# Turned keys copied ahead of the exponents, the merge spread through the last projection of the scan branch, and its buffers placed anew

## The chip, the cores and the metric

The kernel runs on one core of one Trainium2 chip. Five engines share the work: TensorE (PE) does the matrix products, VectorE (DVE), ScalarE (ACT) and GpSimd (POOL) do the elementwise work, and SyncE (SP) issues most transfers; ACT and POOL can issue transfers too, each on a queue of its own. The metric is the device time of one execution in microseconds. The kernel before takes 1907.57 us, the median of three runs from 1902.23 to 1909.16.

## The reference

One layer of a hybrid decoder: 512 prompt tokens and 64 sample tokens (8 sequences of 8) go through the same weights, each group with its own past. Cut to what matters here:

```python
h = x + 0.5 * swiglu(rmsnorm(x))                      # FFN 1
z, xbc, dt, q, k, v, f, g_ssd, g_att = split(rmsnorm(h) @ w_in)
y_ssd = ssd_branch(z, xbc, dt, ...)                   # conv, scan, gate, norm: 4 groups of 512 channels
y_att = fox_attention(q, k, v, f)                     # with a paged cache of 2048 keys a sequence
merged = sigmoid(g_ssd) * (y_ssd @ w_ssd_proj) + sigmoid(g_att) * (y_att @ w_attn_proj)
h = h + merged @ w_out
y = h + 0.5 * swiglu(rmsnorm(h))                      # FFN 2
```

The outputs are y and the new keys, values, forget logs, scan states and conv rows of both groups.

## The kernel before

**Tiles.** All 576 tokens are worked on together, and an activation is kept turned: 8 tiles of 128 channels by 576 tokens. A product is made column tile by column tile (`j`, 128 output channels) and in two halves of 288 tokens. Each operand is split into a high and a low part, so one product is three matmuls for every 128 rows of the weight (`mm3`, L208 to L210: high times high, high times low, low times high). Weights arrive by SP's queue in tiles `stage` (512 KB, four buffers); `split` makes `whi` on ACT (L173) and `wlo` on DVE, or on POOL at every `share[0]`-th time (L174). Activations are split by `hilo`: the high part on ACT (L217), the low part on DVE (L218).

**What sets the order.** The program is written in one sequence and a scheduler orders each engine's instructions by a timeline model of its own; what stands in a `soon()` block gets a higher priority. An engine then runs its instructions in that fixed order and waits wherever an operand is not there. Pools of buffers ("left" and "right" side of the on-chip memory) tie later tiles to the release of earlier ones.

**Stages.** FFN 1; the input projection; the attention, whose sample part turns gathered keys on PE and copies them out of PSUM on ACT (`turn_keys`, L907 and L908: `kT`), in turn with ACT's exponents (L850 for the prompt); then four groups of the scan branch. A group has its conv tiles (`conv_tile`, buffers `xr`), its scan (`group_scan`, which leaves the gated result split in `ygh` and `ygl`), and its projection:

`group_out(g)` multiplies the group's four channel tiles by 512 rows of `w_ssd_proj`: for each of 8 columns and 2 halves 12 matmuls into a PSUM tile `acc` (two banks), then `u = acc * rg` on DVE (L1378) and `accs[j] += u` (L1380; on POOL in groups 1 and 2, on DVE in group 3). `accs0` to `accs7` are the running sums over the groups, 128x576 each. `gate_tile` leaves the gates of the scan branch in DRAM (`thD`), three of them behind group 0's scan and five behind group 3's. The attention's gated projection lies in DRAM too (`mattD`), as does the residual (`hD`).

**The merge**, behind the last `group_out` (L1397 to L1424). For each column it loads the gate `th` on SP's queue (L1403) and the attention part `mt` on ACT's queue (L1405), makes `th = (th + 1) * accs[j]` on DVE (L1406), adds `mt` on POOL (L1407; on DVE for the last column) and splits the sum into `mh` and `ml`. Every one of these tiles lies in a pool that opens when the pools of the scan have closed. The eight residual tiles `h` are loaded on ACT's queue (L1410) into a pool of their own. Then `w_out`: 384 matmuls (8 columns, 2 halves, 8 row tiles, 3 each) that use `mh` and `ml`, and `h = 0.5 * acc + h` on DVE (L1421). For these, PSUM tiles are taken from `acc` and `pv` by turns, so four are there, and the scheduler lets the first four halves (columns 0 and 1) run abreast: they take the row tiles `mh0`, `mh1`, ... in the order in which these are made, and cannot end before the last of the eight is there. FFN 2 follows, with the norm of the new `h`.

Of the kernel before, what the change touches and what calls it, by code (L numbers as in the profile page):

```python
# [93 lines left out]
def build(ctx, tc, A, O):  # L94
# [8 lines left out]
    def pool(name, bufs=1, **kw):  # L103
        return tc.tile_pool(name=name, bufs=bufs, **kw)
# [534 lines left out]
    with pool("att", side="right", reuse_waits="tile") as ap:  # L639
# [242 lines left out]
        class Sample:  # L882
# [17 lines left out]
            def turn_keys(self, jq):  # L900
                kk = self.kk.pop(jq)
                self.kT = []
                for p in range(2):
                    self.kT.append(tl(ap, [P, 512], tag="kT", bufs=2))
                    t = tr()
                    for i in range(4):
                        nc.tensor.transpose(t[:, i * P:(i + 1) * P], kk[:, i, p * P:(p + 1) * P], ident)  # L907
                    act(self.kT[p], t, AF.Copy)  # L908

            def q(self, kv):  # L910
                return qz[:, kv // 2, self.b, kv % 2].rearrange("d g t -> d (g t)")
# [184 lines left out]
                G.tensor_copy(yt[p * 4 + g][:, NP:], ys[:, p, g, :])  # L1096


    xzs = ExitStack()
    xz = xzs.enter_context(pool("xz", side="right", reuse_waits="tile"))  # L1100

# [1 line left out]

    def conv_tile(ct, w, prev, out):

        xr = tl(xz, XR, tag="xr", bufs=2)
        xsamp = xr[:, 3 + NP:]
        xsamp = xsamp.rearrange("p (b u) -> p b u", u=T + 3)
        G.memset(xr[:, :3], 0.0)
        G.tensor_copy(xsamp[:, :, :3], prev.rearrange("p (j b) -> p b j", b=B))  # L1110
        a = acc()
        mm3(a, w, xs, 0)
        with soon():
            V.tensor_tensor(xr[:, 3:3 + HT], a, rbc[:, hs(0)], ALU.mult)
        full = tl(accp, [P, 512], tag="acc")
        a = full[:, :HT]
        mm3(a, w, xs, 1)
        with soon():
            V.tensor_tensor(xr[:, 3 + HT:3 + NP], a[:, :NP - HT], rbc[:, HT:NP], ALU.mult)
        with soon():  # L1120
            V.tensor_tensor(xsamp[:, :, 3:], a[:, NP - HT:].rearrange("p (b t) -> p b t", t=T),
                            rbc[:, NP:].rearrange("p (b t) -> p b t", t=T), ALU.mult)

        n = 3 + (T + 3) * B
        with soon():
            t = full[:n, 512 - P:]
            nc.tensor.transpose(t, xr[:, NP:], ident)
            tt = tl(xz, [n, P], tag="tt", bufs=1)
            act(tt, t, AF.Copy)  # L1129
        nc.scalar.dma_start(out=O["conv_p"][0, 0, :, ct * P:(ct + 1) * P], in_=tt[:3])  # L1130
        for j in range(3):
            r = 3 + T + j
            nc.scalar.dma_start(out=O["conv_s"][0, :, j, ct * P:(ct + 1) * P], in_=tt[r:r + (T + 3) * (B - 1) + 1:T + 3])

        m = NP + B * (T + 3)
        cv = tl(mixp, XR, tag="kf", bufs=2)
        wc = lambda j: P2[:, j * 24 + ct:j * 24 + ct + 1]
        act(cv[:, :m], xr[:, :m], AF.Identity, bias=P1[:, 40 + ct:41 + ct], scale=wc(0))
        for j in range(1, 4):
            V.scalar_tensor_tensor(cv[:, :m], xr[:, j:j + m], wc(j), cv[:, :m], ALU.mult, ALU.add)  # L1140
        act(xr[:, :m], cv[:, :m], AF.Tanh)
        V.scalar_tensor_tensor(out[:, :NP], xr[:, :NP], 1.0, cv[:, :NP], ALU.add, ALU.mult)
        samples = lambda v: v[:, NP + 3:].rearrange("p (b u) -> p b u", u=T + 3)[:, :, :T]
        V.scalar_tensor_tensor(out[:, NP:].rearrange("p (b t) -> p b t", t=T), samples(xr), 1.0, samples(cv), ALU.add, ALU.mult)
# [44 lines left out]
                nc.scalar.dma_start(out=mattD[:, j, :], in_=mt)  # L1189


    sa = mixes.enter_context(pool("ssdacc", reuse_waits="tile"))
    with xzs, pool("ssd", side="right", reuse_waits="tile") as wk:
        accs = [tl(sa, [P, NT], tag=f"accs{j}") for j in range(8)]
        cz = tl(wk, [P, B, 32], tag="cz")
        lastb = tl(wk, [P, 5, 32], tag="x4", bufs=3)
# [10 lines left out]
        def group_scan(g, bT, cT, xg):  # L1207
# [21 lines left out]
            def halves(half):  # L1229

                for i in range(4):
                    if half == 0:
                        yhl.append((tl(wk, [P, NT], F32R, tag="ygh", bufs=4), tl(wk, [P, NT], F32R, tag="ygl", bufs=4)))
                    w = P1[:, 24 + 4 * g + i:25 + 4 * g + i]
                    hi, lo = yhl[i][0][:, hs(half)], yhl[i][1][:, hs(half)]
                    act(hi, xg[:, i, hs(half)], AF.Copy, scale=w)
                    V.scalar_tensor_tensor(lo, xg[:, i, hs(half)], w, hi.bitcast(F32), ALU.mult, ALU.subtract)
# [126 lines left out]
        def group_out(g, ysq, ys_):  # L1364
# [3 lines left out]
            for j in range(8):  # L1368
                w = cw.get(j)
                for half in range(2):  # L1370
                    a = acc()
                    mm3(a, w, ys_, half)
                    if g == 0:
                        with soon():
                            V.tensor_tensor(accs[j][:, hs(half)], a, rg[:, hs(half)], ALU.mult)
                    else:
                        u = tl(wk, [P, HT], tag="u", bufs=2)
                        V.tensor_tensor(u, a, rg[:, hs(half)], ALU.mult)  # L1378
                        E = V if g == 3 else G
                        E.tensor_tensor(accs[j][:, hs(half)], accs[j][:, hs(half)], u, ALU.add)  # L1380

        gs = Cols(win, CGS)
        late = iter(range(8))
        for g in range(4):
# [5 lines left out]
            for _ in range((3, 0, 0, 5)[g]):  # L1390
                j = next(late)
                gate_tile(gs, j, 8 + j)
            group_out(g, *gated)


    hp2 = ctx.enter_context(pool("h2", side="right", reuse_waits="tile"))
    hts = [tl(hp2, [P, NT], tag=f"h{k}") for k in range(8)]  # L1397
    with mixes:
        with pool("mhl", bufs=8, side="right", reuse_waits="tile") as mp, pool("mg", side="right", reuse_waits="tile") as mg:
            mhl = []  # L1400
            for j in range(8):
                th = tl(mg, [P, NT], tag="th", bufs=3)
                nc.sync.dma_start(out=th, in_=thD[:, 8 + j, :])  # L1403
                mt = tl(mg, [P, NT], tag="mt", bufs=3)
                nc.scalar.dma_start(out=mt, in_=mattD[:, j, :])  # L1405
                V.scalar_tensor_tensor(th, th, 1.0, accs[j], ALU.add, ALU.mult)  # L1406
                (G if j < 7 else V).tensor_tensor(th, th, mt, ALU.add)  # L1407
                mhl.append(hilo(mp, th, "mh", "ml"))
            for j in range(8):
                nc.scalar.dma_start(out=hts[j], in_=hD[:, j, :])  # L1410
            wide[0] = True
            co = Cols(A["w_out"][0], 0)
            nrm3 = Norm(16, mg)
            for j in range(8):
                w = co.get(j)
                for half in range(2):
                    a = acc()
                    mm3(a, w, mhl, half)
                    hv = hts[j][:, hs(half)]
                    with soon():  # L1420
                        V.scalar_tensor_tensor(hv, a, 0.5, hv, ALU.mult, ALU.add)  # L1421
                nrm3.add(hts[j])
            nrm3.finish()
            share[0] = 0  # L1424


    with pool("out", bufs=2, reuse_waits="tile") as op:
# [48 lines left out]
```

## Time and profile before

| | value |
|---|---|
| median of three runs | 1907.57 us |
| the profiled execution's own time | 1901.34 us |
| its span, first to last instruction | 1899.5 us |
| last projection of the scan branch, merge, first four halves of `w_out` | 1367 to 1440 us in the span |
| FFN 2 behind it | to the end of the span |

A row of the timeline has the start in us from the span's start, the duration, the engine, the source line, the operation, what is written and read, and in brackets the idle time ahead of it and what ended that. A row by groups has line, engine, operation, operands and count, then the busy time and the mean nanoseconds of one, then the idle time ahead of the group's instructions and who ended it. A row of windows has the stretch and its length, the busy time of PE, of PE's weight loads, DVE, ACT and POOL with the number of instructions, the clock that TensorE was granted (1.00 is full), the busy share of the transfer engines and the bytes moved. The chain is followed back from the last instruction to whatever released each step; its rows give the idle time in us, the count and the longest one.

### The profile page before, as it was taken

How to read it: one execution, taken by the hardware profiler on the slowest of the kernel's cores; microseconds unless marked ns; L12 is line 12 of the kernel's file. 1: busy time of each engine (PE TensorE's matmuls, PEld its weight loads, DVE VectorE, ACT ScalarE, POOL GpSimd, SP SyncE). 2: the span in 40 equal slices, each digit the busy share in tenths (PEclk: the TensorE clock that was granted, in tenths of full speed). 3: DMA queues.
4: the chain of work that ended last, by engine and by line, in shares of the span. 5: the costliest groups of instructions: out<-in, count | busy, mean ns of one | idle time of the engine just before them, and what ended most of it. 6: DMA issues, size and time to landing. Idle time of an engine off the chain costs nothing.

```text
span 1899.5 us, 38775 instructions
## 1 busy us (share of the span) xinstructions
PE 1843.6 (97%) x15335; PEld 1738.3 (92%) x15335; DVE 1061.9 (56%) x2308; ACT 745.5 (39%) x1545; POOL 603.7 (32%) x678
## 2 busy tenths in 40 slices
PE   7999999999999999999899999999979999999999
PEld 7999999999899888888898898888979999999998
DVE  5544234443425677776746968787665545445442
ACT  4233223333323555554425645555423333223322
POOL 0432002312312334433224644747434322102210
PEclk9999999999998999999999999999989999999999
DMA  5453443444625678785456445344543444444432
GB/s 153 111 142 123 134 128 118 122 140 140 158 80 147 187 225 244 213 227 155 115 134 190 148 126 144 104 133 123 165 144 109 132 128 139 132 139 123 121 116 69
DMA packets 298235, 269.71 MB, mean 142 GB/s; under 512 B 55068, under 2 KB 262092, under 8 KB 297900
## 3 DMA queue, kind: packets, MB, share of 16 engines
q1 hardware_dynamic: 230864, 186.52, 35.0%
q10 hardware_dynamic: 57828, 46.09, 7.9%
q0 software_dynamic: 9360, 34.61, 5.9%
q8 instruction: 121, 1.98, 0.4%
q14 instruction: 62, 0.51, 0.1%
HBM read 223.71 MB, written 38.73 MB: 138 GB/s over the span
## 4 chain that ended last, share of the span: by engine, by line
PE 85%; DVE 5%; DMA 4%; ACT 3%; issue 1%; POOL 1%; ACTq 1%; SPq 0%; POOLq 0%; DVEq 0%
PE acc L208 17%; PE acc L209 16%; PE acc L210 16%; PE pv L209 7%; PE pv L208 7%; PE pv L210 7%; PE tr L917 2%; PE tr L907 1%; PE mm L844 1%; DMA ab<-cumD 1%; PE pv L875 1%; PE mm L862 1%; PE pv L1299 1%; DVE kf L1140 1%; PE pv L955 1%
## 5 line engine op out<-in xcount | busy, mean ns | idle before, releaser
L173 ACT ACTIVATE whi<-stage 128x512 fp32r<-128x512 f32 (+2 forms) x474 | 294.8, 622 | 739.4 <-PE acc L209 650.5
L208 PE MATMUL acc<-xh,whi 128*128 128x288 f32 x1792 | 544.7, 304 | 9.0 <-ACT tt L1129 3.8
L209 PE MATMUL acc<-xl,whi 128*128 128x288 f32 x1792 | 535.8, 299 | 0.0
L210 PE MATMUL acc<-xh,wlo 128*128 128x288 f32 x1792 | 535.0, 299 | 0.0
L174 DVE TENSOR_TENSOR wlo<-stage,whi 128x512 fp32r<-128x512 f32 (+1 forms) x373 | 261.1, 700 | 263.3 <-ACT whi L173 249.4
L208 PEld LDWEIGHTS acc<-xh,whi 128*128 128x128 f32 x1792 | 341.1, 190 | 15.4 <-ACT tt L1129 6.7
L209 PEld LDWEIGHTS acc<-xl,whi 128*128 128x128 f32 x1792 | 341.3, 190 | 1.9 <-issue 1.4
L210 PEld LDWEIGHTS acc<-xh,wlo 128*128 128x128 f32 x1792 | 340.7, 190 | 1.8 <-issue 1.2
L174 POOL TENSOR_TENSOR wlo<-stage,whi 128x512 fp32r<-128x512 f32 (+1 forms) x101 | 138.2, 1368 | 315.8 <-ACT whi L173 300.4
L341 POOL TENSOR_TENSOR u<-u,s 128x288 f32<-128x288 f32 x88 | 81.3, 924 | 425.6 <-DVE u L340 379.9
L208 PE MATMUL pv<-xh,whi 128*128 128x288 f32 (+1 forms) x720 | 214.1, 298 | 1.0 <-ACT xh L220 0.9
L209 PE MATMUL pv<-xl,whi 128*128 128x288 f32 (+1 forms) x720 | 212.9, 296 | 0.0
L210 PE MATMUL pv<-xh,wlo 128*128 128x288 f32 (+1 forms) x720 | 212.4, 295 | 0.0
L208 PEld LDWEIGHTS pv<-xh,whi 128*128 128x128 f32 (+1 forms) x720 | 135.1, 188 | 1.7 <-ACT xh L220 1.1
L209 PEld LDWEIGHTS pv<-xl,whi 128*128 128x128 f32 (+1 forms) x720 | 135.1, 188 | 1.2
L210 PEld LDWEIGHTS pv<-xh,wlo 128*128 128x128 f32 (+1 forms) x720 | 135.0, 188 | 0.2
L208 PE MATMUL pv<-hh,whi 128*128 128x288 f32 x352 | 105.7, 300 | 0.0
L343 POOL TENSOR_TENSOR hl<-u,hh 128x288 fp32r<-128x288 f32 x88 | 79.1, 901 | 80.7 <-ACT hh L342 80.7
L208 PE MATMUL acc<-hh,whi 128*128 128x288 f32 x352 | 104.1, 296 | 0.0
L209 PE MATMUL pv<-hl,whi 128*128 128x288 f32 x352 | 104.0, 296 | 0.0
L210 PE MATMUL acc<-hh,wlo 128*128 128x288 f32 x352 | 104.0, 296 | 0.0
L209 PE MATMUL acc<-hl,whi 128*128 128x288 f32 x352 | 104.0, 295 | 0.0
(346 smaller groups left out, 3622.5 us busy)
## 6 DMA issues: line engine op xcount, KB each, us to landing
stage<-in_w_in_dram SPq DMA_DIRECT2D x52, 512.0 KB
stage<-in_ffn_w_up_dram SPq DMA_DIRECT2D x44, 512.0 KB
stage<-in_ffn_w_gate_dram SPq DMA_DIRECT2D x43, 512.0 KB
stage<-in_ffn_w_down_dram SPq DMA_DIRECT2D x40, 512.0 KB
h<-in_state_ssm_dram SPq DMA_DIRECT2D x64, 256.0 KB
hTD<-hT ACTq DMA_DIRECT2D x32, 256.0 KB
pb<-pastD SPq DMA_DIRECT2D x32, 256.0 KB
ab<-cumD SPq DMA_DIRECT2D x32, 256.0 KB
```

The lines of the kernel that those rows point to most:

```text
L173: act(hi, view, AF.Copy)
L174: e.tensor_tensor(lo, view, hi.bitcast(F32), ALU.subtract)
L208: mm(out, lhsT=hi, rhs=a, start=first and i == 0, stop=False)
L209: mm(out, lhsT=hi, rhs=b, start=False, stop=False)
L210: mm(out, lhsT=lo, rhs=a, start=False, stop=last and i == n - 1)
L341: G.tensor_tensor(u, u, sil[half], ALU.mult)
L343: G.tensor_tensor(hl[:, hs(half)], u, hh[:, hs(half)].bitcast(F32), ALU.subtract)
L844: mm(s[:, :n], lhsT=q, rhs=ks[2 * self.p + e][:, :n], start=hl == 0, stop=hl == 1)
L862: nc.tensor.transpose(t[:, j * P:(j + 1) * P], lt[:, j * P:(j + 1) * P], ident)
L875: mm(self.ob[o:o + 32, i * P:(i + 1) * P], lhsT=vtok[j][:, v0:v0 + 32], rhs=self.pts[e][:, j * P:(j + 1) * P], start=j == 0, stop=j == i)
L907: nc.tensor.transpose(t[:, i * P:(i + 1) * P], kk[:, i, p * P:(p + 1) * P], ident)
L917: mm(s[kv * 32:(kv + 1) * 32, :], lhsT=self.q(kv), rhs=self.kT[kv // 2], start=True, stop=True)
```

## The change

Four things.

1. The copies `kT` are written under `soon()`.
2. The sums `accs` and the row sums `ssq` move into a pool `sums` on the right side that opens before the conv's pool and stays to the end. The pool of the projection's operands (`outs`: `ygh`, `ygl`, `u`) is split from the scan's and lives as long as the conv's pool. `xr` has three buffers, not two.
3. The gates and attention parts are loaded into the conv's old tiles (`bT`, `cT` and `xr`), both on ACT's queue, and those of columns 0 and 1 are asked for ahead of the last `group_out`. As the merge needs no new pool but the one of `mh` and `ml`, the scheduler is free to set a column's merge between later columns of the projection.
4. The residual tiles take the places of the sums: `h` for column j is loaded into `accs[j]`'s place when the merge has read it, on POOL's queue, behind the addition of that column.

The lines of the change have new numbers: the merge's two elementwise operations are L1415 and L1416, the loads L1387, L1389 and L1419, `u` and the sums L1380 and L1382, the residual's addition L1430.

```diff
--- before.py
+++ after.py
@@ -905,7 +905,8 @@
                     t = tr()
                     for i in range(4):
                         nc.tensor.transpose(t[:, i * P:(i + 1) * P], kk[:, i, p * P:(p + 1) * P], ident)
-                    act(self.kT[p], t, AF.Copy)
+                    with soon():
+                        act(self.kT[p], t, AF.Copy)
 
             def q(self, kv):
                 return qz[:, kv // 2, self.b, kv % 2].rearrange("d g t -> d (g t)")
@@ -1096,6 +1097,7 @@
                 G.tensor_copy(yt[p * 4 + g][:, NP:], ys[:, p, g, :])
 
 
+    sa = ctx.enter_context(pool("sums", side="right", reuse_waits="tile"))
     xzs = ExitStack()
     xz = xzs.enter_context(pool("xz", side="right", reuse_waits="tile"))
 
@@ -1103,7 +1105,7 @@
 
     def conv_tile(ct, w, prev, out):
 
-        xr = tl(xz, XR, tag="xr", bufs=2)
+        xr = tl(xz, XR, tag="xr", bufs=3)
         xsamp = xr[:, 3 + NP:]
         xsamp = xsamp.rearrange("p (b u) -> p b u", u=T + 3)
         G.memset(xr[:, :3], 0.0)
@@ -1189,8 +1191,8 @@
                 nc.scalar.dma_start(out=mattD[:, j, :], in_=mt)
 
 
-    sa = mixes.enter_context(pool("ssdacc", reuse_waits="tile"))
-    with xzs, pool("ssd", side="right", reuse_waits="tile") as wk:
+    wo = xzs.enter_context(pool("outs", side="right", reuse_waits="tile"))
+    with pool("ssd", side="right", reuse_waits="tile") as wk:
         accs = [tl(sa, [P, NT], tag=f"accs{j}") for j in range(8)]
         cz = tl(wk, [P, B, 32], tag="cz")
         lastb = tl(wk, [P, 5, 32], tag="x4", bufs=3)
@@ -1230,7 +1232,7 @@
 
                 for i in range(4):
                     if half == 0:
-                        yhl.append((tl(wk, [P, NT], F32R, tag="ygh", bufs=4), tl(wk, [P, NT], F32R, tag="ygl", bufs=4)))
+                        yhl.append((tl(wo, [P, NT], F32R, tag="ygh", bufs=4), tl(wo, [P, NT], F32R, tag="ygl", bufs=4)))
                     w = P1[:, 24 + 4 * g + i:25 + 4 * g + i]
                     hi, lo = yhl[i][0][:, hs(half)], yhl[i][1][:, hs(half)]
                     act(hi, xg[:, i, hs(half)], AF.Copy, scale=w)
@@ -1374,10 +1376,18 @@
                         with soon():
                             V.tensor_tensor(accs[j][:, hs(half)], a, rg[:, hs(half)], ALU.mult)
                     else:
-                        u = tl(wk, [P, HT], tag="u", bufs=2)
+                        u = tl(wo, [P, HT], tag="u", bufs=2)
                         V.tensor_tensor(u, a, rg[:, hs(half)], ALU.mult)
                         E = V if g == 3 else G
                         E.tensor_tensor(accs[j][:, hs(half)], accs[j][:, hs(half)], u, ALU.add)
+
+        def merge_load(j):
+
+            th = tl(xz, [P, NT], tag="cT" if j % 2 else "bT", bufs=2)
+            nc.scalar.dma_start(out=th, in_=thD[:, 8 + j, :])
+            mt = tl(xz, XR, tag="xr", bufs=3)[:, :NT]
+            nc.scalar.dma_start(out=mt, in_=mattD[:, j, :])
+            return th, mt
 
         gs = Cols(win, CGS)
         late = iter(range(8))
@@ -1390,38 +1400,37 @@
             for _ in range((3, 0, 0, 5)[g]):
                 j = next(late)
                 gate_tile(gs, j, 8 + j)
-            group_out(g, *gated)
-
-
-    hp2 = ctx.enter_context(pool("h2", side="right", reuse_waits="tile"))
-    hts = [tl(hp2, [P, NT], tag=f"h{k}") for k in range(8)]
-    with mixes:
-        with pool("mhl", bufs=8, side="right", reuse_waits="tile") as mp, pool("mg", side="right", reuse_waits="tile") as mg:
-            mhl = []
-            for j in range(8):
-                th = tl(mg, [P, NT], tag="th", bufs=3)
-                nc.sync.dma_start(out=th, in_=thD[:, 8 + j, :])
-                mt = tl(mg, [P, NT], tag="mt", bufs=3)
-                nc.scalar.dma_start(out=mt, in_=mattD[:, j, :])
-                V.scalar_tensor_tensor(th, th, 1.0, accs[j], ALU.add, ALU.mult)
-                (G if j < 7 else V).tensor_tensor(th, th, mt, ALU.add)
-                mhl.append(hilo(mp, th, "mh", "ml"))
-            for j in range(8):
-                nc.scalar.dma_start(out=hts[j], in_=hD[:, j, :])
-            wide[0] = True
-            co = Cols(A["w_out"][0], 0)
-            nrm3 = Norm(16, mg)
-            for j in range(8):
-                w = co.get(j)
-                for half in range(2):
-                    a = acc()
-                    mm3(a, w, mhl, half)
-                    hv = hts[j][:, hs(half)]
-                    with soon():
-                        V.scalar_tensor_tensor(hv, a, 0.5, hv, ALU.mult, ALU.add)
-                nrm3.add(hts[j])
-            nrm3.finish()
-            share[0] = 0
+            if g < 3:
+                group_out(g, *gated)
+    merging = [merge_load(j) for j in range(2)]
+    group_out(3, *gated)
+
+
+    with mixes, xzs, pool("mhl", bufs=8, side="right", reuse_waits="tile") as mp:
+        mhl, hts = [], []
+        for j in range(8):
+            if j > 1:
+                merging.append(merge_load(j))
+            th, mt = merging[j]
+            V.scalar_tensor_tensor(th, th, 1.0, accs[j], ALU.add, ALU.mult)
+            (G if j < 7 else V).tensor_tensor(th, th, mt, ALU.add)
+            mhl.append(hilo(mp, th, "mh", "ml"))
+            hts.append(tl(sa, [P, NT], tag=f"accs{j}"))
+            nc.gpsimd.dma_start(out=hts[j], in_=hD[:, j, :])
+        wide[0] = True
+        co = Cols(A["w_out"][0], 0)
+        nrm3 = Norm(16, mp)
+        for j in range(8):
+            w = co.get(j)
+            for half in range(2):
+                a = acc()
+                mm3(a, w, mhl, half)
+                hv = hts[j][:, hs(half)]
+                with soon():
+                    V.scalar_tensor_tensor(hv, a, 0.5, hv, ALU.mult, ALU.add)
+            nrm3.add(hts[j])
+        nrm3.finish()
+        share[0] = 0
 
 
     with pool("out", bufs=2, reuse_waits="tile") as op:
```

**What stands where on DVE.** At the first two columns of the last `group_out`. The names: `u` and `accs` as above, `ssq` holds `rg`, `th` is the gate's tile, which after the change is called `bT` or `cT`. Before, the sums of all eight columns stand in one piece, and the merge behind the last of them:

```order
L1378 TENSOR_TENSOR u_17731<-acc_17718,ssq_16663 128x288
L1380 TENSOR_TENSOR accs_2343_12683<-accs_2343_12683,u_17731 128x288
L1378 TENSOR_TENSOR u_17747<-acc_17734,ssq_16663 128x288
L1380 TENSOR_TENSOR accs_2343_12683<-accs_2343_12683,u_17747 128x288
L1406 SCALAR_TENSOR_TENSOR th_17769<-th_17769,accs_2336_12676 128x576
L1406 SCALAR_TENSOR_TENSOR th_17779<-th_17779,accs_2337_12677 128x576
L218 TENSOR_TENSOR ml_17776<-th_17769,mh_17775 128x576
L1406 SCALAR_TENSOR_TENSOR th_17789<-th_17789,accs_2338_12678 128x576
L218 TENSOR_TENSOR ml_17786<-th_17779,mh_17785 128x576
```

Now, from column 0's second sum on (columns 0 to 2):

```order
L1382 TENSOR_TENSOR accs_2336_12679<-accs_2336_12679,u_17501 128x288
L174 TENSOR_TENSOR wlo_17617<-stage_17614,whi_17616 128x512
L1415 SCALAR_TENSOR_TENSOR bT_17434<-bT_17434,accs_2336_12679 128x576
L1380 TENSOR_TENSOR u_17521<-acc_17508,ssq_16666 128x288
L1382 TENSOR_TENSOR accs_2337_12680<-accs_2337_12680,u_17521 128x288
L1380 TENSOR_TENSOR u_17537<-acc_17524,ssq_16666 128x288
L1382 TENSOR_TENSOR accs_2337_12680<-accs_2337_12680,u_17537 128x288
L1415 SCALAR_TENSOR_TENSOR cT_17438<-cT_17438,accs_2337_12680 128x576
L1380 TENSOR_TENSOR u_17559<-acc_17546,ssq_16666 128x288
L218 TENSOR_TENSOR ml_17768<-bT_17434,mh_17767 128x576
```

A column's merge now stands right behind its sums, and its `ml` one column later, in between the `u` that empty PSUM.

**What stands where on POOL.** Between the conv's and scan's work of group 3 and FFN 2. Before, the halves of the weights come first and the merge's additions behind them, without a transfer:

```order
L174 TENSOR_TENSOR wlo_17715<-stage_17676,whi_17714 128x512
L174 TENSOR_TENSOR wlo_17866<-stage_17859,whi_17865 128x512
L174 TENSOR_TENSOR wlo_17932<-stage_17859,whi_17931 128x512
L1407 TENSOR_TENSOR th_17769<-th_17769,mt_17771 128x576
L1407 TENSOR_TENSOR th_17779<-th_17779,mt_17781 128x576
L1407 TENSOR_TENSOR th_17789<-th_17789,mt_17791 128x576
```

Now:

```order
L1416 TENSOR_TENSOR bT_17434<-bT_17434,xr_17436 128x576
L1419 DMA accs_3260_17771<-hD_78 128x576
L174 TENSOR_TENSOR wlo_17653<-stage_17614,whi_17652 128x512
L1416 TENSOR_TENSOR cT_17438<-cT_17438,xr_17440 128x576
L1419 DMA accs_3263_17779<-hD_78 128x576
L1416 TENSOR_TENSOR bT_17781<-bT_17781,xr_17783 128x576
L1419 DMA accs_3268_17791<-hD_78 128x576
L174 TENSOR_TENSOR wlo_17727<-stage_17688,whi_17726 128x512
```

Additions, residual loads and weight halves alternate; there are eight loads in all, the last behind seven additions.

**What stands where on PE.** At the end of the last `group_out`. Before, its 192 matmuls are in one piece, and `w_out` follows with four halves abreast:

```order
L209 MATMUL acc_17734<-ygl_16981,whi_17714 128x288
L210 MATMUL acc_17734<-ygh_16980,wlo_17715 128x288
L208 MATMUL pv_17869<-mh_17775,whi_17861 128x288
L208 MATMUL acc_17895<-mh_17775,whi_17861 128x288
L208 MATMUL pv_17935<-mh_17775,whi_17927 128x288
L208 MATMUL acc_17961<-mh_17775,whi_17927 128x288
```

Now a half of `w_out` begins behind 132 of the 192 (eleven halves of sixteen), and the two alternate:

```order
L209 MATMUL pv_17865<-ml_17768,whi_17857 128x288
L208 MATMUL acc_17672<-ygh_16971,whi_17652 128x288
L209 MATMUL acc_17672<-ygl_16972,whi_17652 128x288
L210 MATMUL acc_17672<-ygh_16971,wlo_17653 128x288
L208 MATMUL acc_17672<-ygh_16975,whi_17652 128x288
```

The first matmul that needs the last column's `ml` was the 269th from the beginning of the last `group_out`, and is now the 272nd. ACT's queue carries the gate and attention loads of columns 0 and 1 during group 3, and the later ones between the `mh`; SP's queue has eight transfers fewer. Of the 64 `kT` copies one has another place (one exponent earlier, at the attention's start), and 63 stand where they stood. The program orders of FFN 1, of most of the attention and of FFN 2 are as before; in the tails of the groups some instructions of the conv change places with their neighbours.

## The prediction

> **What bounds the kernel now.** The first page of the profile says which engine sets the time, and where it doesn't.
>
> ```profile
> PE 1843.6 (97%) x15335; PEld 1738.3 (92%) x15335; DVE 1061.9 (56%) x2308; ACT 745.5 (39%) x1545; POOL 603.7 (32%) x678
> PE   7999999999999999999899999999979999999999
> PEclk9999999999998999999999999999989999999999
> PE 85%; DVE 5%; DMA 4%; ACT 3%; issue 1%; POOL 1%; ACTq 1%; SPq 0%; POOLq 0%; DVEq 0%
> ```
>
> PE is busy for 97% of the span and carries 85% of the chain. Of the 40 slices one late in the program falls to 7 tenths, the slice from about 1377 to 1425 us. Only what shortens PE's waits can shorten the time, so the next view is the chain's waits that end on PE.
>
> ```profile
> PE pv L208 <- ACT mh L217: 9.8, 4, 8.1
> PE tr L917 <- ACT kT L908: 5.8, 7, 1.1
> ```
>
> Both belong to the change: PE waits 9.8 us in four waits for the merge's `mh`, one of them 8.1 us long, and 5.8 us in seven waits for `kT`. The windows show the first place whole.
>
> ```profile
> core 0: us, PE busy (x) PEld busy (x) DVE busy (x) ACT busy (x) POOL busy (x), PEclk, DMA share, GB/s
> 1367.00:1392.70 25.70, 25.70 (x195) 25.62 (x194) 16.64 (x36) 5.68 (x9) 5.67 (x4) 1.00 0.29 91
> 1392.70:1421.10 28.40, 17.10 (x81) 14.61 (x80) 19.81 (x20) 7.25 (x11) 14.75 (x9) 0.76 0.67 203
> 1421.10:1462.00 40.90, 40.90 (x310) 40.90 (x309) 21.68 (x32) 17.68 (x28) 16.86 (x11) 1.00 0.26 80
> ```
>
> Ahead of it and behind it PE is never idle and needs 25.70/195 = 0.132 us a matmul. Between, 28.4 us hold 81 matmuls, 10.7 us at that pace. **17.7 us** are lost there: waits, and a lower clock (0.76). The timeline names the waits.
>
> ```profile
> 1395.54 0.76 DVE L1406 SCALAR_TENSOR_TENSOR th<-th,accs 128x576 f32<-128x576 f32 x1 [1.70 <-DMA th<-thD]
> 1398.83 2.75 POOL L1407 TENSOR_TENSOR th<-th,mt 128x576 f32<-128x576 f32 x2 [3.86 <-DMA mt<-mattD]
> 1400.99 0.61 PE L208 MATMUL pv<-mh,whi 128*128 128x288 f32 x1 [8.13 <-ACT mh L217]
> 1419.68 1.60 DVE L218 TENSOR_TENSOR ml<-th,mh 128x576 fp32r<-128x576 f32 x2
> 1421.17 0.29 PE L209 MATMUL acc<-ml,whi 128*128 128x288 f32 x1
> ```
>
> The loads of the gates and the attention part arrive about 1395.5 and 1398.8, after PE ran dry. From there the merge itself is the limit, up to the last `ml` at 1421.28 (1419.68 plus 1.60).
>
> **What the merge's engines are worth.** Two pairs of rows decide the sum.
>
> ```profile
> 1407.11 1.43 POOL L1407 TENSOR_TENSOR th<-th,mt 128x576 f32<-128x576 f32 x1 [2.31 <-DVE th L1406]
> 1407.32 1.83 DVE L1406 SCALAR_TENSOR_TENSOR th<-th,accs 128x576 f32<-128x576 f32 x1 [0.34 <-DMA th<-thD]
> 1409.28 2.04 POOL L1407 TENSOR_TENSOR th<-th,mt 128x576 f32<-128x576 f32 x1 [0.75 <-ACT mh L217]
> 1409.29 0.76 DVE L218 TENSOR_TENSOR ml<-th,mh 128x576 fp32r<-128x576 f32 x1
> 1374.42 1.46 POOL L174 TENSOR_TENSOR wlo<-stage,whi 128x512 fp32r<-128x512 f32 x1 [5.07 <-ACT whi L173]
> 1375.38 0.46 DVE L1378 TENSOR_TENSOR u<-acc,ssq 128x288 f32<-128x288 f32 x1 [0.65 <-PE acc L210]
> ```
>
> DVE's operation begun inside POOL's takes 1.83 us where the same one alone took 0.76 (1395.54), and ends at 1409.15, 0.61 behind POOL's end at 1408.54. POOL's, begun with DVE's, takes 2.04: DVE's 0.76 and **1.28** of its own. The two engines exclude each other. But `u`, with one operand in PSUM, takes its usual 0.46 inside POOL's operation. So DVE's work on two on-chip operands and POOL's work add up as if one engine did both. The rows by groups give the sizes.
>
> ```profile
> L1380 DVE TENSOR_TENSOR accs<-accs,u 128x288 f32<-128x288 f32 x16 | 7.3, 458 | 0.6
> L1378 DVE TENSOR_TENSOR u<-acc,ssq 128x288 f32<-128x288 f32 x16 | 7.3, 457 | 8.4 <-PE acc L210 8.2
> L1407 DVE TENSOR_TENSOR th<-th,mt 128x576 f32<-128x576 f32 x1 | 0.8, 759 | 0.0
> L1407 POOL TENSOR_TENSOR th<-th,mt 128x576 f32<-128x576 f32 x7 | 11.6, 1669 | 10.1 <-DMA mt<-mattD 3.9 <-DVE th L1406 3.7 <-ACT mh L217 1.5
> L174 POOL TENSOR_TENSOR wlo<-stage,whi 128x512 fp32r<-128x512 f32 (+1 forms) x101 | 138.2, 1368 | 315.8 <-ACT whi L173 300.4
> L174 DVE TENSOR_TENSOR wlo<-stage,whi 128x512 fp32r<-128x512 f32 (+1 forms) x373 | 261.1, 700 | 263.3 <-ACT whi L173 249.4
> ```
>
> A test on before: from 1395.54 to 1421.28, 25.74 us, lie eight `th`, eight `ml` and one addition at 0.76 and one `wlo` at 0.70 on DVE, 13.6 us, and seven additions at 1.28 and one `wlo` at 1.37 on POOL, 10.3 us. Together 23.9 us, **93%** of the stretch: the pair of engines is the merge's limit, not its transfers.
>
> **The merge, part by part.** The change removes the late loads' wait and lets the merge begin under the last projection. By the order given above, between column 0's first sum and the last `ml` DVE now does 16 sums (7.3), eight `th` and eight `ml` (12.2), one addition (0.8), five `wlo` (3.5): 23.8 us; POOL seven additions (9.0) and four `wlo` (5.5): 14.4 us. The sum, 38.2 us, at 93% takes 41.1. The 16 `u` (7.3 us) may lie under POOL's operations, but POOL's 14.4 us fill only about two thirds of the 21 that DVE's 23.8 leave of the stretch, and a `u` comes when PE has a tile done, not when POOL runs. I count half, 3.7. That gives 44.8 us, with the ends 41.1 (all covered) and 48.4 (none).
>
> ```profile
> 1369.51 0.46 DVE L1380 TENSOR_TENSOR accs<-accs,u 128x288 f32<-128x288 f32 x1
> ```
>
> From 1369.51 the last `ml` comes at **1414.3** (1410.6 to 1417.9), against 1421.28: 7.0 us earlier (3.4 to 10.7). It is the 272nd matmul that needs it, no longer the 269th, so three more are done by then: 0.4. Gain 7.4. PE alone would be there after 271 x 0.132 = 35.8 us, at about 1403 from 1367.2, so it still waits some 11 us, now in many short gaps: a late `u` holds one of the two PSUM banks.
>
> **The clock in those gaps.**
>
> ```profile
> 1150.00:1160.00 10.00, 8.16 (x69) 7.24 (x66) 8.37 (x16) 6.66 (x20) 5.47 (x7) 0.83 0.59 159
> 1410.00:1420.00 10.00, 7.21 (x36) 5.86 (x36) 9.84 (x9) 3.40 (x6) 6.57 (x4) 0.87 0.42 116
> 1401.40 0.44 PE L208 MATMUL acc<-mh,whi 128*128 128x288 f32 x1
> 1401.64 0.44 PE L208 MATMUL pv<-mh,whi 128*128 128x288 f32 x1
> ```
>
> Stretches with PE busy for 7 to 8 of 10 us have 0.83 and 0.87, and after the 8.13 us gap matmuls start 0.24 us apart, not 0.132: about half speed. A mean of 0.83 is then some 3.4 us of the 10 at half speed. Where PE waits for `ml` anyway, a lower clock is free. Only a dip in the last microseconds counts: 3.4/0.24 = 14 matmuls lose 14 x 0.108 = **1.5 us**, my choice between no dip and two (3.0). The Trainium skill ("TensorE: Matmul & The Clock Gate", "HAM oscillation — how this bites in real kernels") puts the bite at idle gaps over about 3.4 us; by it gaps as short as mine cost nothing and the gain would be 1.5 us larger. The two rows above, without a gap that long in the second, speak against it.
>
> **The residual loads on POOL.** They leave ACT's queue for POOL's, eight issues between the additions. Before has no plain transfer on POOL in this stretch; the nearest is the gather.
>
> ```profile
> L801 POOL DMA_INDIRECT kk<-in_cache_k_dram,pidx x32: 936/952/1128, 502.8 to 860.3; - x32
> ```
>
> At 0.95 us each they occupy POOL for 7.6 us. POOL has 44.8 - 14.4 = 30 us without work of its own, and a load waits only for its column's `th`, which is done before the addition ahead of it. Behind each stand additions that `mh` waits for. I count nothing, with ends 0 and 8.2 us (all eight in series with DVE's and POOL's work, 7.6/0.93). The residual is needed at about 1415 at the earliest; columns 0 and 1 are asked for about 1375. [...]
>
> **The kT copies.** The order moves one of 64 copies, ahead of one exponent.
>
> ```profile
> 623.44 0.72 ACT L850 ACTIVATE L<-L,mn 128x512 f32<-128x512 f32 x1
> 624.07 0.19 ACT L850 ACTIVATION_READ_ACCUMULATOR L<-L,mn 128x1 f32 x1
> ```
>
> That takes at most 0.72 + 0.19 = 0.9 us off a wait of PE; I count half, **0.5**. The 5.8 us of the chain stay otherwise.
>
> **The rest.** The third `xr` buffer moves conv instructions and loads in the groups' tails by a place or two, on DVE too, while the count of instructions stays. I count 0, with ends of 2 us either way. The loads on ACT's queue stand ahead of group 3's end, where the row of 1367 shows ACT busy for 5.68 of 25.7 us. SP loses eight transfers and brings `w_out`'s weights sooner: covered, since PE waits for `ml` then.
>
> **The sum.** 7.4 - 1.5 + 0.5 = **6.4 us**. Against the profiled execution (1901.34, a span of 1899.5 and 1.8 around it) that is 1894.9. The median is 1907.57, and the runs spread over 7 us; against it the sum gives **1901.2**.
>
> **Rivals.** (a) *The engines' exclusion hardly binds, and PE goes through.* For it: the interleaving puts POOL's operations beside `u` and beside DVE's waits. Then all 17.7 us but the clock's go: 16 us, 1891.5. Against it is the 93%. Halfway, with `u` covered and no dip, it is 10.7 + 0.4 + 0.5 = 11.6, 1896.0. (b) *Slower: POOL's queue becomes the bound.* The addition of column j+1 stands behind the load of column j, and `mh`, `ml` and PE wait for it. If an issue holds DVE up as an addition does, the stretch is (38.2 + 8 x issue)/0.93 + 3.7, and passes before's 51.8 us (1369.51 to 1421.28) from an issue of 0.8 us on. At the gather's 0.95 it is 52.9, and the gain becomes -1.1 + 0.4 - 1.5 + 0.5 = -1.7: 1909.3. At 2 us it is 62.0, and 10.8 us are lost: 1918.4. For it: 0.95 is over 0.8. Against it: a gather reads a list that a plain load doesn't have, and nothing shows that issuing excludes DVE. (c) *The change doesn't do what it says:* `kT` is such a case already, with 0.9 us at most. For the merge it would be so if a `th` came late again; the loads of columns 2 to 7 are issued between the `mh`, two columns ahead, and a landing takes some us. If every column waited for its transfer as column 0 did (1.70), the 7.4 us would be gone: 1907.
>
> **Chances.** About what a measurement of this kernel can tell from no change is 0.5%, 9.5 us. The forecast lies within it. Forecast with its ends (gain 2 to 9.5): 0.47; (a) and its halfway case: 0.36, faster by over 0.5%; (c): 0.07, same; (b): 0.10, of which a little stays within 0.5%. So faster 0.36, same 0.55, slower 0.09. The range reaches to (a) almost and to (c): 1889 to 1909.
>
> **What would show it.** Right: the last `ml` 44.8 us behind the first sum, no gap of 8 us on PE, rows of DVE that end shortly behind POOL's, the matmuls of `w_out` between those of the projection, seven waits for `kT` as before. Wrong: a POOL row in which an issue takes over 0.8 us; `u` that waits behind `th`; a clock below 0.9 after 1415; groups 1 to 3 longer by more than 2 us.

## The result, and the profile after

The changed kernel takes 1893.01 us, the median of 20 runs (1883.92 to 1901.95), against 1907.03 us for 20 runs of the kernel before (1896.25 to 1912.45). The ratio is 0.993, with a 95% interval from 0.9914 to 0.9945: **13.3 us faster** (10.5 to 16.4); that is the difference of the means, the medians are 14.0 apart. The forecast was 1901.2 us in a range from 1889 to 1909, a gain of 6.4 us: the sign and the range hold, the size is half of what came.

The profiled execution took 1897.44 us, span 1895.6, which is only 3.9 less than the span before. It lies 4.4 us over its kernel's median and the one before lay 5.7 us under its own, so the gain has to be read stage by stage. Both executions are timed at the same places of the program:

| us from the span's start | before | changed | changed takes |
|---|---|---|---|
| first score matmul of the attention | 606.2 | 609.1 | +2.9 |
| last score matmul | 882.0 | 890.3 | +5.4 |
| first `accs` sum of the last `group_out` | 1369.5 | 1377.2 | -0.6 |
| end of the last `ml` | 1421.3 | 1416.2 | **-12.7** |
| end of the span | 1899.5 | 1895.6 | +1.2 |

The change's place is the fourth row. The page's first lines and the slices of the changed kernel:

```profile
PE 1842.9 (97%) x15335; PEld 1734.7 (92%) x15335; DVE 1067.4 (56%) x2308; ACT 746.0 (39%) x1545; POOL 606.0 (32%) x686
PE   8999999999999999999999999999999999999998
PEclk9999999999997999999999999999999999999999
```

The slice of 7 tenths is gone. The waits that end on PE, over the whole span (first row) and from 1377 to 1417 us (the other two), with the idle time in us, the count and the longest:

```profile
PE tr L918 <- ACT kT L909: 5.7, 6, 1.1
...
PE acc L208 <- DVE u L1380: 3.8, 4, 1.2
PE pv L209 <- DVE ml L218: 0.6, 1, 0.6
```

The waits for `kT` are what they were (5.8 us before). The wait of 8.1 us for `mh` has left the list, and 3.8 us of waiting for `u` have come, in gaps of at most 1.2. The window of the stretch from the first sum to the end of the last `ml` in the changed kernel, columns as in the prediction's windows:

```profile
1377.19:1416.23 39.04, 34.63 (x251) 33.33 (x251) 37.86 (x53) 11.19 (x17) 20.35 (x19) 1.00 0.65 201
```

And the kernel before over the same instructions:

```profile
1369.51:1421.28 51.77, 40.47 (x256) 37.91 (x256) 35.67 (x53) 11.68 (x18) 19.13 (x12) 0.87 0.48 148
```

DVE now works for 37.86 of 39.04 us: it is the bound, as forecast. PE idles for 4.4 us, where I had forecast some 11, and its clock stays at 1.00. The timeline shows the exclusion between DVE and POOL at work:

```profile
1380.43 0.45 DVE L1380 TENSOR_TENSOR u<-acc,ssq 128x288 f32<-128x288 f32 x1
1380.91 1.42 DVE L1382 TENSOR_TENSOR accs<-accs,u 128x288 f32<-128x288 f32 x1
...
1385.30 1.83 DVE L218 TENSOR_TENSOR ml<-bT,mh 128x576 fp32r<-128x576 f32 x1
...
1388.38 0.45 DVE L1382 TENSOR_TENSOR accs<-accs,u 128x288 f32<-128x288 f32 x1
1388.75 0.44 DVE L1380 TENSOR_TENSOR u<-acc,ssq 128x288 f32<-128x288 f32 x1
1389.12 0.74 DVE L1415 SCALAR_TENSOR_TENSOR bT<-bT,accs 128x576 f32<-128x576 f32 x1
1389.78 0.44 DVE L1382 TENSOR_TENSOR accs<-accs,u 128x288 f32<-128x288 f32 x1
```

```profile
1380.59 1.42 POOL L1416 TENSOR_TENSOR bT<-bT,xr 128x576 f32<-128x576 f32 x1 [3.55 <-DVE bT L1415]
1381.96 0.61 POOL L1419 DMA_DIRECT2D accs<-hD  x1
1382.59 1.30 POOL L174 TENSOR_TENSOR wlo<-stage,whi 128x512 fp32r<-128x512 f32 x1
1385.09 1.42 POOL L1416 TENSOR_TENSOR cT<-cT,xr 128x576 f32<-128x576 f32 x1 [1.20 <-DVE cT L1415]
```

POOL's addition runs from 1380.59 to 1382.01. `u`, with one operand in PSUM, keeps its 0.45 beside it; the sum that follows takes 1.42 and ends at 1382.33, 0.32 behind POOL. The `ml` at 1385.30 fares alike. POOL's issue of a load at 1381.96 doesn't hold the sum up: it ends in the middle of the issue. And where POOL rests (1388.38 to 1389.78), DVE's rows of 0.44 begin 0.37 apart and the one of 0.74 is followed after 0.66: **a row overlaps the next one's start by some 0.07 us.** The rows by groups over the stretch:

```profile
L1382 DVE TENSOR_TENSOR accs<-accs,u 128x288 f32<-128x288 f32 x16 | 14.5, 907 | 0.3
L1380 DVE TENSOR_TENSOR u<-acc,ssq 128x288 f32<-128x288 f32 x15 | 6.7, 446 | 0.6 <-PE acc L210 0.6
L218 DVE TENSOR_TENSOR ml<-cT,mh 128x576 fp32r<-128x576 f32 x4 | 5.5, 1370 | 0.2 <-ACT mh L217 0.2
L218 DVE TENSOR_TENSOR ml<-bT,mh 128x576 fp32r<-128x576 f32 x4 | 4.1, 1018 | 0.0
L174 DVE TENSOR_TENSOR wlo<-stage,whi 128x512 fp32r<-128x512 f32 x5 | 3.4, 679 | 0.0
L1415 DVE SCALAR_TENSOR_TENSOR cT<-cT,accs 128x576 f32<-128x576 f32 x4 | 3.0, 754 | 0.1
L1415 DVE SCALAR_TENSOR_TENSOR bT<-bT,accs 128x576 f32<-128x576 f32 x4 | 3.0, 745 | 0.0
L1416 DVE TENSOR_TENSOR cT<-cT,xr 128x576 f32<-128x576 f32 x1 | 0.8, 751 | 0.0
```

The sums take 14.5 us where they need 16 x 0.445 = 7.1, the `ml` 9.6 where they need 6.0: 7.4 + 3.6 = 11.0 us of DVE's time pass behind POOL. `u` loses nothing, and neither do the `th` (0.75 us each).

How much of the stretch's 12.7 us is left further on shows the addition of the last half of `w_out`, before and changed:

```profile
1461.81 0.46 DVE L1421 SCALAR_TENSOR_TENSOR h<-acc,h 128x288 f32<-128x288 f32 x1 [0.38 <-PE acc L210]
```

```profile
1457.47 0.46 DVE L1430 SCALAR_TENSOR_TENSOR accs<-acc,accs 128x288 f32<-128x288 f32 x1 [0.38 <-PE acc L210]
```

From the first sum these are 92.3 and 80.3 us: **12.0 us** gained, within the interval of the runs.

### The profile page after: what moved, and what is told of

Same layout as the page of the kernel before. It is cut to its first block, busy times and chain, and to the rows that moved or that the text cites. A ratio compares the mean times of both kernels' runs of the same rounds, so it can differ in the third digit from the quotient of the medians.

```text
span 1895.6 us, 38765 instructions
## 1 busy us (share of the span) xinstructions
PE 1842.9 (97%) x15335; PEld 1734.7 (92%) x15335; DVE 1067.4 (56%) x2308; ACT 746.0 (39%) x1545; POOL 606.0 (32%) x686
## 4 chain that ended last, share of the span: by engine, by line
PE 84%; DVE 6%; DMA 4%; ACT 3%; issue 2%; POOL 1%; ACTq 0%; SPq 0%; DVEq 0%; POOLq 0%
PE acc L208 16%; PE acc L209 16%; PE acc L210 16%; PE pv L209 7%; PE pv L208 7%; PE pv L210 7%; PE tr L918 2%; PE tr L907 1%; PE mm L844 1%; PE pv L875 1%; PE pv L1301 1%; PE mm L862 1%; DMA ab<-cumD 1%; PE tr L376 1%; PE pv L956 1%
```

## The experiments

The theory: the merge's work, laid between the columns of the projection, is the gain, and DVE's rows with the time that POOL blocks them set the new stretch. The rivals: the loads and places are the gain, not the order; or POOL's own row is what the merge waits for; or the `kT` copies and the third `xr` have a share. Each kernel's stretch is read like the two rows above (first sum to end of the last `ml`). It is steady: 39.04, 39.01 and 39.00 us in the three kernels that leave it as changed, 51.77 and 52.11 in the two that leave it as before, while whole times of one kernel spread over 10 us and more.

**The order taken away** (merge_last):

```diff
+        one = tl(mp, [P, 1], tag="one", bufs=1)
+        V.tensor_scalar(one, accs[7][:, NT - 1:], 0.0, 1.0, ALU.mult, ALU.add)
-            V.scalar_tensor_tensor(th, th, 1.0, accs[j], ALU.add, ALU.mult)
+            V.scalar_tensor_tensor(th, th, one, accs[j], ALU.add, ALU.mult)
```

> The changed kernel, but every column's (th + 1) * accs takes its 1 from a small tile that is made from the last column's sum, so no merge can begin before the last sum; loads, places and queues stay as changed. Stretch from the first sum of the last group_out to the end of the last ml: 51.8 us before, 39.0 us changed. If the interleaving is what was gained: about 23.5 us of sums and then some 25 us of merge, 48 to 50 us, so 2 to 3 us are left of the gain (ratio to before 0.998 to 0.999). If the early loads and the new places are what was gained: the stretch stays near 40 us and the ratio near 0.993.

Measured: 1905.39 us, ratio 1.0006 (0.9986 to 1.0025). Its window:

```profile
1373.57:1423.71 50.14, 38.80 (x255) 37.30 (x254) 38.87 (x54) 11.58 (x18) 22.87 (x20) 0.87 0.55 170
```

Of its waits on PE, the longest:

```profile
PE pv L208 <- ACT mh L217: 5.5, 1, 5.5
```

The stretch is 50.14 us, just above the 48 to 50 expected, with the hole back. The loads of columns 0 and 1 are early, the places are the new ones, and the gain is gone: the order is what brings it. (Reading the 1 from a tile makes the eight `th` slower, 0.81 us in place of 0.75 where POOL rests: some 0.5 us in all, by these rows.) One thing more hangs on the order: with two `th` tiles of each name, the loads of columns 4 to 7 wait for the `ml` of columns 0 to 3, which come late here.

**The additions on DVE** (adds_dve): `(G if j < 7 else V).tensor_tensor(th, th, mt, ALU.add)` becomes `V.tensor_tensor(...)`.

> The changed kernel with all eight merge additions on DVE, none on POOL. If DVE and POOL exclude each other: the 7 additions add 7 x 0.67 = 4.7 us of DVE's own work and take away about as much blocked time (the sums and ml that took 1.1 to 2.0 us instead of 0.44 and 0.75), so the stretch stays within 37.5 to 40 us of 39.0 and the time within 2 us of the changed kernel's. If the two engines work side by side and the long rows had another reason: DVE has 4.7 us more, stretch about 43.5 us, ratio to before about 0.9955.

Measured: 1888.57 us, ratio 0.9915 (0.9889 to 0.9941). Its window:

```profile
1369.97:1404.78 34.81, 33.79 (x251) 33.16 (x251) 34.01 (x60) 11.26 (x18) 12.88 (x13) 1.00 0.76 229
```

The sums in its rows by groups:

```profile
L1382 DVE TENSOR_TENSOR accs<-accs,u 128x288 f32<-128x288 f32 x16 | 8.7, 552 | 0.1
```

DVE has seven instructions more, and the stretch is 4.2 us shorter, below the 37.5 to 40 that I expected under the exclusion: the sums fall from 14.5 to 8.7 us, `ml` to 6.0 (four at 746 and four at 745 ns). This speaks for the exclusion against engines that work side by side, and more strongly than I had put it. PE is busy for 33.79 of 34.81 us and DVE for 34.01, and PE's waits for `u` have fallen from 3.8 to 1.0: a quicker DVE could bring no more than that. POOL now waits for DVE: one of its `wlo` took 3.82 us, where 1.29 is usual. And the issues of the loads, which are left on POOL, can be seen apart from its additions. One of them ran from 1386.11 for 0.54 us; on DVE stood:

```profile
1386.11 0.44 DVE L1382 TENSOR_TENSOR accs<-accs,u 128x288 f32<-128x288 f32 x1
1386.47 0.74 DVE L218 TENSOR_TENSOR ml<-bT,mh 128x576 fp32r<-128x576 f32 x1
```

A sum and an `ml`, both with two on-chip operands, begin inside this issue and take their usual time.

**The residual loads on SP's queue** (h_sync): `nc.gpsimd.dma_start(out=hts[j], ...)` becomes `nc.sync.dma_start(...)`.

> The changed kernel with the eight residual loads on SP's queue, none on POOL. If DVE's work sets the stretch and an issue on POOL costs nothing: 39.0 us within 1 us, ratio within 0.001 of the changed kernel's 0.993. If POOL's row is what the merge waits for: 8 x 0.57 us go, stretch 35 to 36 us, ratio about 0.991. If an issue on SP's queue holds up w_out's weights instead: longer than 40 us.

Measured: 1888.38 us, ratio 0.9918 (0.989 to 0.9946).

```profile
1364.79:1402.40 37.61, 34.06 (x247) 32.76 (x247) 36.46 (x53) 11.17 (x17) 17.25 (x11) 1.00 0.69 208
```

1.4 us shorter, between the two expectations: shared among the eight issues, one costs the merge 0.18 us of its 0.56. DVE stays the bound (36.46 of 37.61).

**Both** (dve_sync):

> The changed kernel with all merge additions on DVE and the residual loads on SP's queue: POOL keeps only weight halves. The additions alone brought the stretch from 39.0 to 34.8 us, with PE busy for 33.8 of them; the loads alone brought it to 37.6. If PE is the bound now, the two don't add up: 34.2 to 34.8 us, ratio 0.991 to 0.992 as with the additions alone. If DVE still sets it and each issue on POOL costs DVE 0.18 us: 33.4 us, ratio 0.9905.

Measured: 1890.12 us, ratio 0.9913 (0.9887 to 0.9939), stretch 34.82 us. The two do not add up: with the additions on DVE the issues on POOL cost nothing (34.81 us with them).

**Additions on DVE and sums 576 wide** (wide_dve):

```diff
+                        V.tensor_tensor(u[:, hs(half)], a, rg[:, hs(half)], ALU.mult)
+                        if half:
+                            V.tensor_tensor(accs[j], accs[j], u, ALU.add)
```

> The changed kernel with all merge additions on DVE and the last group's sums made 576 wide, eight instead of sixteen. If DVE sets the stretch: 8 x (2 x 0.41 - 0.67) = 1.2 us less than the kernel with the additions on DVE, 36.5 to 38.5 us, close to PE's own 35.8 us for the 271 matmuls; time 1 to 2.5 us under the changed kernel (ratio about 0.992). If something else sets it (PE's PSUM banks, the weights): 39 us or more, no gain.

Measured: 1890.67 us, ratio 0.9916 (0.9892 to 0.9939), 34.41 us from the first sum to the end of the last `ml`. But the first sum now waits for both halves of its column, so this stretch begins a half later than in the other kernels. From the group's first `u` to the end of the last `ml` it took 36.50 us (1382.27 to 1418.77), against 35.30 with the additions alone (1369.48 to 1404.78): 1.2 us longer, where 1.2 less was expected. Why is open. Nothing is gained in the whole time. In its profiled execution the part ahead (first `xr` to the group's first `u`) took 452.9 us against 450.1; TensorE's clock was at 0.50 for 13.7 us of it, against 6.8 to 10.2 us in the other kernels.

**The old merge with its additions on DVE** (before_dve), the same edit in the kernel before:

> The kernel before with all eight merge additions on DVE; nothing else of the change. If the old merge was limited by DVE and POOL excluding each other: seven additions of 1.28 us on POOL become seven of 0.67 us on DVE, and DVE's rows of 1.8 to 2.0 us go; 4 to 5 us less, stretch from the first sum to the last ml 46.5 to 48 us in place of 51.8, ratio about 0.9975. If its transfers were the limit: 51 to 52 us, ratio 1.000.

Measured: 1902.89 us, ratio 0.999 (0.9969 to 1.0011).

```profile
1372.45:1422.76 50.31, 38.91 (x252) 38.20 (x252) 35.42 (x60) 11.68 (x18) 7.52 (x5) 0.83 0.49 153
```

50.31 us, 1.5 less, not 4 to 5. So the old merge was not limited by the exclusion, or not by it alone, though its work filled 93% of the time: with it gone, waits for loads and for the chain of one column take its place. The two longest of DVE's waits in the merge:

```profile
1398.44 0.76 DVE L1406 SCALAR_TENSOR_TENSOR th<-th,accs 128x576 f32<-128x576 f32 x1 [1.65 <-DMA th<-thD]
1402.05 0.76 DVE L1407 TENSOR_TENSOR th<-th,mt 128x576 f32<-128x576 f32 x1 [2.85 <-DMA mt<-mattD]
```

**No order, additions on DVE** (last_dve), both edits in the changed kernel:

> The kernel of merge_last (no merge before the last sum) with all merge additions on DVE as well. merge_last alone brought the stretch from 51.8 to 50.1 us, the additions on DVE alone (in the kernel before) to 50.3. If each of the old merge's two limits, late loads and the exclusion, stood behind the other: both away give more than the sum of 3.2 us, 44 to 46 us. If the two are separate parts of the stretch: 48 to 49 us. In either case more than the 34.8 us that the interleaved kernel with the additions on DVE has; were it near 35, the interleaving would not be the cause of the gain.

Measured: 1898.76 us, ratio 0.999 (0.9964 to 1.0016). Its window:

```profile
1360.10:1408.58 48.48, 38.14 (x262) 36.44 (x261) 36.11 (x61) 11.32 (x18) 12.27 (x13) 0.93 0.53 169
```

And one row of DVE's timeline:

```profile
1395.44 0.76 DVE L1418 TENSOR_TENSOR cT<-cT,xr 128x576 f32<-128x576 f32 x1 [3.05 <-DMA xr<-mattD]
```

48.48 us: the savings stand side by side (50.14 less 1.7), and DVE waits 3.05 us for a single load. With the merge in the columns the same kernel has 34.81. That difference, 13.7 us, is the order's, with what hangs on it: the late loads of the columns behind the first ones are part of it.

**kT** (kt_only is the kernel before with `soon()` on the copies, no_kt the changed one without):

> The kernel before with the kT copies written under soon() and nothing else. By the order one copy of 64 moves: at most 0.9 us gained, ratio 0.9995 to 1.0, and PE's waits for kT stay at 5 to 6 us. If the copies in front delay the exponents (the attention of the changed kernel's profiled execution took 281.2 us from the first score matmul to the last, 275.8 us before): the attention is some 5 us longer and the ratio about 1.003.

> The changed kernel without soon() on the kT copies. Same as the changed kernel within 1 us (ratio to before about 0.993) if the copies matter little; 5 us better (0.990) if they cost the attention what the profiled execution seems to show; 1 to 3 us worse (0.994) if they gain there.

Measured: 1906.75 us, ratio 1.0005 (0.9984 to 1.0025), and 1893.64 us, ratio 0.9933 (0.99 to 0.9966). PE's waits for `kT` are 5.0 and 5.5 us; over all twelve kernels they lie between 5.0 and 6.4, with the edit and without. The attention took 279.8 and 277.9 us. Over all kernels it took 275.8 to 277.9 without the edit (three executions) and 274.3 to 281.2 with it (nine): too much spread to tell a microsecond or two, and no loss of 5 us that goes with the edit.

**Two xr buffers** (xr2):

> The changed kernel with two xr buffers, as before, not three; the merge's mt then has two. If the third buffer only reorders the groups' tails: ratio within 0.001 of the changed kernel's 0.993, groups 1 to 3 equally long. If it is a gain or a loss of its own: 2 us either way, in the stretch from the first conv tile to the last group's first sum (448.7 us before, 448.3 us changed).

Measured: 1891.22 us, ratio 0.9911 (0.9886 to 0.9936), stretch 39.00 us. From the first `xr` to the last group's first sum it took 450.9 us (448.3 changed, 448.9 before, 446.7 to 450.6 in the others but wide_dve). The whole time shows no loss: the third buffer is worth nothing that these runs could tell.

## Why the prediction was right in its mechanism and short in its size

**What held.** The place, PE's hole in the merge. The mechanism: interleaving, with DVE as the new bound, `u` unharmed beside POOL, DVE's two-operand rows blocked. The term of the exclusion: I had POOL's 14.4 us less 3.7, that is 10.7 us on DVE's path; 11.0 were measured. That the two agree so well is in part luck: POOL's elementwise rows took 16.2 us, some of it waiting for DVE, and 2.4 us of `u` lay under them, not 3.7. `kT`: one copy moved, no change in its waits; the 0.5 us that I had booked for it can't be told from the spread. The rest of the program: no change outside the spread. Rival (a), by which the exclusion hardly binds, fell with these 11.0 us. The rival of a POOL row that turns slow fell: an issue took 0.56 us, not the gather's 0.95, and only 0.18 of it reached the merge; the price at which it decides was 0.8. By the rows the issues take no part in the exclusion: the eight took 0.55 to 0.61 us each with DVE busy beside them, and with the additions gone from POOL DVE's rows begin inside them at their usual length. The Trainium skill ("SBUF — State Buffer", "Who interferes with whom") reports the same for the operation of these rows: beside `tensor_tensor` a transfer issued on POOL did not stall, beside `tensor_copy` it did. The trace agrees (0.44 us for the sum that began with an issue at 1386.11).

**The chances.** By my own mark of 0.5% the result, 0.7% faster, is clear of noise. It fell in the case to which I had given 0.36; I had favoured a gain of 2 to 9.5 us, with 0.47. The range held because it reached further, almost to rival (a).

**What was mis-sized: the 44.8 us of the merge, part by part.** Measured were 39.0, which is below the lower end I gave (41.1). Term by term:

| us | predicted | measured |
|---|---|---|
| DVE's own rows, `u` among them | 31.1 | 30.0 |
| blocked by POOL | 10.7 | 11.0 |
| allowance for waiting | 2.9 | 1.2 |
| overlap of one row with the next | 0 | -3.1 |
| stretch | 44.7 | 39.1 |

The measured column comes from the group rows of the stretch: all of DVE's durations add up to 41.0 us (30.0 and 11.0), but it is busy for 37.86 of the time, so 3.1 lie on top of each other; 39.04 less 37.86 is idle. The sums miss 44.8 and 39.04 by rounding. Of the 1.1 us in the first row, half is the first `u`, which stands ahead of the stretch: 15 of the 16 lie in it. The two wrong terms:

- *Durations instead of distances.* I added up durations of rows. In a packed stretch one row begins before the last one ends, by 0.06 us a row on 53 rows. A `u` and its own sum stand 0.48 apart (1380.43 and 1380.91), and that sum reads that `u`; rows that don't need each other stand 0.37 apart.
- *The 93%.* I took what the old merge's work left over, 7%, as the price of the exclusion, and carried it to the new stretch. before_dve shows that the old merge had other limits of nearly the same height. The new stretch, full of work that doesn't hang together, has hardly any such waits: DVE idles for 3% of it.

**The clock** was the other wrong step: -1.5 us for a dip in the gaps. The windows of the changed kernel:

```profile
1380.00:1390.00 10.00, 8.53 (x62) 8.08 (x61) 9.90 (x15) 2.95 (x5) 5.25 (x6) 1.00 0.59 181
1390.00:1400.00 10.00, 7.70 (x57) 7.23 (x56) 9.96 (x15) 2.95 (x5) 6.21 (x6) 1.00 0.77 249
1400.00:1410.00 10.00, 9.37 (x69) 8.97 (x68) 9.86 (x14) 2.65 (x4) 6.09 (x6) 1.00 0.49 141
```

PE busy for 7.70 of 10 us, and a clock of 1.00: the busy share of a window of 10 us doesn't tell its clock. That no gap here is longer than 1.2 us agrees with the rule of the Trainium skill ("TensorE: Matmul & The Clock Gate", "HAM oscillation — how this bites in real kernels") that I had set against my rows: gaps over some 3.4 us bite. But the kernel before doesn't fit it: no gap of its windows of 1150 to 1160 and 1410 to 1420 is longer than 1.84 us, and both have the lower clock. The traces show more than I had read in them. The clock that they record is 1.00 or 0.50 and changes only at the ends of steps of 3.41 us, and what PE did in one step goes with the clock of the next:

| step of 3.41 us | PE busy in it, us | clock of the next step |
|---|---|---|
| before, from 1151.25 | 1.57 | 0.50 |
| before, from 1393.60 (in the gap of 8.13 us) | 0.00 | 0.50 |
| before, from 1414.08 (gaps of 0.67 and 1.46 us) | 1.28 | 0.50 |
| changed, from 1389.60 (the least busy of the stretch) | 2.21 | 1.00 |

Over the twelve traces, from 120 to 1885 us, the clock falls 42 times. In 33 of these falls PE had been busy for 0 to 49% of the step ahead; only four steps with so little work (46 to 48%) kept the full clock. The other nine lie just ahead of the attention, with PE busy throughout, and stay open. So gaps of 1 us between matmuls left the clock alone here because no step of the new stretch had PE busy for less than 65%: the dip for which I had taken off 1.5 us did not come.

Put right, the sum reads: 51.8 less 39.0 is 12.7, and from the end of the last `ml` to the last half's addition it took 41.2 us where it took 40.5 before. The 0.4 us that I had booked there for three matmuls done earlier did not come; 0.7 were lost. So 12.0 are left in place of 5.9 (7.4 less 1.5). In size this is the case that the prediction gave as halfway to its rival (a), 11.6 us, but not in its reason: that case has all of `u` covered, and 2.4 of its 6.7 us were.

**A version that goes further.** The additions on DVE take another 4.2 us out of the stretch (34.81 for 39.04). In the whole time the ratio is 0.9915 for 0.993, with intervals that overlap: the trace shows the gain, the runs don't prove it.

## What to carry to other kernels

Two elementwise engines that exclude each other, as these do in rows with two on-chip operands, count as one; then moving work to the faster of them pays even where that one is the bound, as seven additions of 1.4 to 1.9 us on POOL became seven of 0.67 us on DVE and 4.2 us went. A chain of load, combine and split that stands behind a matmul loop is worth laying between the loop's columns before its single waits are mended: mending two of them brought 1.5 and 1.6 us, the order 11 to 14. And a packed stretch is summed by the distance from start to start of rows that don't depend on each other, never by durations, with no idle share taken over from a stretch that had other waits.

## What the runs showed of the hardware beyond that

A plain load issued on POOL occupies it for 0.54 to 0.61 us, while DVE's two-operand rows go on beside it. Blocked DVE rows end 0.3 us (128x288) to 0.6 us (128x576) behind POOL's. And the same program differs between executions ahead of any edit: the attention began at 598 to 611 us over the twelve profiled kernels, with the program of the stages ahead of it the same in all. TensorE's clock tells them apart: it stays full there in the three that came first (598.2 to 602.3 us), is at 0.50 for 13.7 us in two (606.2 and 606.3), and for 20.5 us in the other seven (608.2 to 611.1), from 586 to 592 us on; what lowers it there is open. That is as much as the whole change is worth, so a single profiled execution against another one can't weigh it, and a stage can.
